# Query and key products in halves with shifted operands, and three reorderings in a two-layer hybrid decoder kernel

## The chip, the cores and the metric

The kernel runs on one core of a Trainium2 chip. The metric is the device time of one execution in microseconds (us), from the first to the last instruction and a little around them. Three executions of the kernel before took 1192.15, 1189.67 and 1191.78 us; their median is 1191.78.

A core has five engines with a queue of instructions each: TensorE (PE in the profile; its loads of the held operand are counted apart as PEld), VectorE (DVE), ScalarE (ACT), GpSimd (POOL) and SyncE (SP), which here only issues DMA transfers. An engine starts its instructions in the order of its queue and waits at each for the results that it needs. TensorE takes both operands from on-chip memory and writes sums into PSUM.

## The reference, cut to what matters

The inputs are one sequence of 512 tokens with 1024 channels and a conditioning vector `c`. There are two layers; each has a token mixer and then a gated feed-forward part with a convolution, and every part is scaled and shifted by three vectors computed from `c`.

```python
def modulate(x, g, shift, scale):
    return rmsnorm(x, g) * (1.0 + scale) + shift

def s5_mixer(h, ...):                      # layer 0
    u = h @ w_in                           # 1024 -> 1024, 64 groups of 16 channels
    ...                                    # complex diagonal state, 64 per group, scanned over the tokens
    y = gelu(y + d_skip * u)
    y = y * sigmoid(y @ w_glu)
    return y @ w_out

def fox_mixer(h, w_in, b_f, w_out):        # layer 1
    proj = h @ w_in                        # queries, keys, values of 16 heads x 64, and 16 gate columns
    ...                                    # F = cumsum(log_sigmoid(gate + b_f))
    s = q @ k.T / 8 + F[t] - F[s]          # causal, softmax over s
    return softmax(s) @ v @ w_out

def conv_ffn(h, w_up, conv_w, conv_b, w_down):
    a, b = split(h @ w_up)                 # 1024 -> 2 x 2816
    return (silu(causal_conv3(a)) * b) @ w_down

for i in range(2):
    h = h + gate * mixer_i(modulate(h, ...))
    h = h + gate * conv_ffn(modulate(h, ...))
return rmsnorm(h, final_g)
```

All data are float32.

## The kernel before, in words

**Layout.** Activations stand transposed: 1024 channels as 8 tiles (`KT`) of 128 partitions, 512 tokens (`S`) as columns. A large product is computed as three matmuls a tile pair: each operand is split into a high part and a remainder (`hi` and `lo`, both in the fast float32 form), and `hi*hi + hi*lo + lo*hi` is summed in PSUM (`mms`, lines 303 to 310). `put_parts` makes them: ScalarE copies the high part (line 287), VectorE subtracts for the low one (line 292). The products at the start of the state-space layer (lines 1144, 1155 and 1175) and the small ones inside it stay plain float32, one matmul a pair.

**Places in memory.** The normalized input of a product is a pair of tiles `a_hi`, `a_lo`, and a table says how many elements of 4 bytes each is shifted from the start of its room: `WHOLE = {"a_hi": 0, "a_lo": 16}` or `HALF = {"a_hi": 48, "a_lo": 0}` (lines 41 and 42). `norm_mod(i, start)` makes the pair; the default is `WHOLE`. `self.odd` shifts the weights' low part by 32 elements. The up projections of both feed-forward parts use `HALF` and `odd`; the attention layer's input, made by `norm_mod(2)`, uses `WHOLE`.

**`product`** (line 312) runs over output tiles `m`. For each it loads and splits the weights, and then issues the 3 x 8 matmuls over the 512 columns at once, or, with `apart`, over the first 256 columns and then over the second. After each `k` it may call `step`; in the attention layer `step` is `unit`, which issues a piece of the attention work (line 1500 and others) that has fallen due at that count. So attention's matmuls stand between the eight `k` of the query and key products, which are the product over `fox_qk`: 16 tiles, two (queries and keys) for a pair of heads.

**The start.** Line 1114 sums squares for the norm over 512 tokens. `s5_params` then computes, on VectorE, small tables of the state-space layer; a helper called `Ew` logs its operations, and `in_turn` puts two logged lists into one stream so that they are spread evenly over each other. Lines 861 to 864 do this with the inverse root of the norm (`inv_root`, which starts by reading the statistics from PSUM, line 410) and with `s5_turns` (sines and cosines brought to other powers). Line 1130 scales the input by root and gain. The shift vector of the modulation is a product of `c` with a weight matrix that is read as 512 KB pieces (`ada_pe`, line 221; `ada_w` in the transfers); `next(shift)` moves this generator on by one piece, and its last call turns the rows into columns (lines 164 and 169). The first input product (line 1144) uses the input without the shift; the shift's part of it is a column, eight matmuls of one column (line 1155), that ScalarE adds while copying the product out (line 1161, `uf`). From the second input product on (line 1175) the input with the shift is used (line 1164).

**The state-space layer** runs in eight steps `m`. For each, `s5_inputs(m)` makes a 128 x 128 kernel matrix on TensorE (lines 984 and 989), adds `dd`, turns it (line 995, `ktt`), copies it (`kt`, line 996), writes it to a DRAM buffer (`s_z`, line 998) whose other rows are zero, and reads it back in 128 shifted copies (`tw`, line 1001): a 128 x 1024 table. Eight copies multiply this by a causal mask into `t` (line 1007 on ScalarE, line 1005 on GpSimd), one for each position `i` in a block of eight tokens. For the last two tables GpSimd takes some of them: `i` = 2, 5 for table 6 and 0, 2, 5 for table 7. `t` is the operand of the output matmuls of line 1061; those of line 1069 add the part that comes from the states, with tables `w` that VectorE makes (line 958). The outputs go through gelu and are split for the gate's product (lines 1193 and 1194).

**Order.** A scheduler, not the order of the calls alone, sets each engine's queue, so moved code may move its neighbours too.

Of the kernel before, what the change touches and what calls it, by code (L numbers as in the profile page):

```python
# [8 lines left out]
F32 = mybir.dt.float32  # L9
F32R = mybir.dt.float32r  # L10
I32 = mybir.dt.int32
AF = mybir.ActivationFunctionType
# [5 lines left out]
P = 128  # L18
D = 1024
KT = D // P  # L20
S = 512
# [9 lines left out]
NH = 16  # L31
# [32 lines left out]
class Trunk:  # L64
# [247 lines left out]
    def product(self, w, ms, nk, x, evac, head=0, tail=0, after=None, ticks=0, halves=HALVES, tail_pool=(), first=None, step=None, apart=False, ready=(), spare=False):  # L312
# [17 lines left out]
        for m in ms[head:len(ms) - tail]:  # L330
            wk = ready[m] if m in ready else self.weights(w[m], nk)
            ps = self.aux.tile([P, S], F32, name="aux") if spare else self.mm.tile([P, S], F32, name="mmp")
            for c in HALVES if apart else (full,):
                for k in range(nk):
                    self.mms(ps[:, c], wk, x, k, nk, c)
                    if step:
                        step()
            evac(m, ps, full)
            self.tick(ticks)
# [462 lines left out]
class S5(Trunk):  # L802
# [37 lines left out]
    def s5_params(self, pool, tp, prm, stats):  # L840
# [23 lines left out]
        in_turn(*logs)  # L864
# [100 lines left out]

    def s5_inputs(self, m):
# [21 lines left out]
        nc.vector.tensor_tensor(turned, pk[:, 0], dd, ALU.add)  # L988
        for a in range(0, H4, 2):
# [5 lines left out]
        nc.tensor.transpose(pk[:, 1], turned, self.ident)  # L995
        nc.scalar.activation(kt, pk[:, 1], AF.Copy)
        z = self.z[m]
        nc.sync.dma_start(z[:P], kt)
# [4 lines left out]
        for i in range(L):  # L1003
            if m >= KT - 2 and i % 3 == 2 or m == KT - 1 and i == 0:
# [79 lines left out]
    def s5(self, i, nxt):  # L1084
# [4 lines left out]
        with ExitStack() as stack:  # L1089
# [3 lines left out]
            with ExitStack() as start:  # L1093
# [12 lines left out]
                with tc.manual_schedule(engines={ENG.PE, ENG.Activation, ENG.DVE, ENG.SP}):  # L1106
# [29 lines left out]
                    for k in range(KT):  # L1136
# [4 lines left out]
                        if k == 6:  # L1141
                            self.s5_consts(keep, tp)
                            self.s5_signs_b()
                        nc.tensor.matmul(ps, w[0][:, k, :], x[:, k], start=(k == 0), stop=(k == KT - 1))
                    next(shift)
# [7 lines left out]
                    col = self.aux.tile([P, 1], F32, name="aux")  # L1153
                    for k in range(KT):
                        last_mm = nc.tensor.matmul(
# [13 lines left out]
            def inputs(m):  # L1169
                if m:  # L1170
                    if m > 1:
                        load_w(m)
                    ps = self.mm.tile([P, S], F32, name="mmp")
                    for k in range(KT):
# [111 lines left out]
class Kernel(S5):  # L1286
# [98 lines left out]
    def fox_heads(self, pool, x):  # L1385
# [27 lines left out]
        self.product(self.io["fox_qk"], range(NH), KT, x, project, ticks=1, step=self.unit)  # L1413
# [100 lines left out]
def build(tc, io, out, stop=None):  # L1514
    with ExitStack() as ctx:
# [6 lines left out]
        x = k.ffn(1, 0, x, k.norm_mod(2), WHOLE_TILES[0], SUMS, True)  # L1522
# [90 lines left out]
```

## Time and profile before

| What | us |
|---|---|
| three executions | 1192.15, 1189.67, 1191.78 |
| median | 1191.78 |
| profiled execution, its own time | 1192.04 |
| its span, first to last instruction | 1190.3 |
| mean granted clock of TensorE | 0.995 |

| Stage | window | TensorE busy |
|---|---|---|
| norm, tables, modulation | 0 to 26.2 | 17.96 |
| first input products | 26.2 to 65 | 37.96 |
| state-space steps | 65 to 140 | 74.72 |
| last two tables and outputs | 140 to 170 | 24.92 |
| gate and output products | 170 to 262 | 91.14 |
| first feed-forward part | 262 to 638 | 375.10 |
| attention: end of the down projection, values, queries and keys, output | 638 to 850 | 210.19 |
| second feed-forward part | 850 to 1190 | 331.89 |

"Busy" counts time in which an engine has an instruction under way. Matmuls overlap, so a busy TensorE may still run at different paces: the pace is the distance between the starts of two matmuls that follow each other. A group's line in the profile gives line, engine, operation, output and inputs, shape and count; behind the bar stand its busy time and the mean of one in ns, and in brackets the idle time of the engine ahead of it and whose result ended it. The chain of waits goes back from the last instruction, at each step to what released it.

### The profile page before, as it was taken

To read this page: it belongs to the slowest core of one execution; us is meant where nothing else is said; L and a number is where in the kernel's file an instruction comes from. 1 tells how busy PE (TensorE), PEld (TensorE's weight loads), DVE (VectorE), ACT (ScalarE), POOL (GpSimd) and SP (SyncE) were. 2 spreads that over 40 slices of the span, in tenths; PEclk is the share of its full clock that TensorE was granted. 3 is DMA by queue.
4 is the path that set the end of the run, shared out by engine and by line. 5 is a ranking of instruction groups with operands and counts; after the bars stand their busy time and mean duration, and the time that the engine had idled before them with its cause. 6 is when DMAs were issued, how large, how long until landed. Compare 5 with 4: busy or idle time off the path is not lost.

```text
span 1190.3 us, 21170 instructions
## 1 busy us (share of the span) xinstructions
PE 1163.9 (98%) x8183; PEld 1016.3 (85%) x8183; DVE 971.6 (82%) x1813; ACT 639.1 (54%) x1137; POOL 108.8 (9%) x162
## 2 busy tenths in 40 slices
PE   7999989999999999999999999999999999999997
PEld 2456677899999999999999788878999989999987
DVE  8899976889887889876676788866999878888855
ACT  2554525446666666665442666554556545555543
POOL 1000110000011111111000433330000000000000
PEclk9999999999999999999999999999999999999999
DMA  9677758833699898887613555523123332333331
GB/s 360 227 245 250 232 179 292 286 117 108 161 250 257 230 252 235 228 246 200 193 54 127 204 194 177 183 76 108 37 89 103 120 108 87 112 123 108 93 89 71
DMA packets 79427, 202.70 MB, mean 170 GB/s; under 512 B 23919, under 2 KB 26191, under 8 KB 78303
## 3 DMA queue, kind: packets, MB, share of 16 engines
q1 hardware_dynamic: 72847, 181.96, 45.9%
q0 software_dynamic: 6192, 18.88, 9.1%
q8 instruction: 64, 1.05, 0.4%
q10 hardware_dynamic: 288, 0.52, 0.1%
q14 instruction: 36, 0.29, 0.1%
HBM read 194.41 MB, written 6.92 MB: 169 GB/s over the span
## 4 chain that ended last, share of the span: by engine, by line
PE 72%; DVE 15%; DMA 6%; issue 3%; ACT 3%; POOL 1%; SPq 0%; DVEq 0%; POOLq 0%; ACTq 0%
PE mmp L308 35%; PE mmp L568 12%; PE aux L568 5%; DVE w_lo L292 4%; PE mmp L1354 3%; PE mmp L1175 3%; DMA raw<-in_w_up 3%; DVE sums L539 2%; PE mmp L1205 2%; DVE conv L622 2%; PE aux L1500 2%; PE aux L1483 1%; PE aux L1061 1%; PE aux L1069 1%; DVE nm_t L539 1%
## 5 line engine op out<-in xcount | busy, mean ns | idle before, releaser
L287 ACT ACTIVATE w_hi<-raw 128x1024 fp32r<-128x1024 f32 (+4 forms) x197 | 173.3, 888 | 126.2 <-PE mmp L308 60.9
L292 DVE TENSOR_TENSOR w_lo<-raw,w_hi 128x1024 fp32r<-128x1024 f32 (+4 forms) x154 | 155.7, 1013 | 30.9 <-ACT w_hi L287 27.0
L308 PE MATMUL mmp<-ghi,w_hi 128*128 128x512 f32 (+1 forms) x392 | 144.1, 368 | 0.0
L308 PE MATMUL mmp<-glo,w_hi 128*128 128x512 f32 (+1 forms) x392 | 143.7, 367 | 0.0
L308 PE MATMUL mmp<-ghi,w_lo 128*128 128x512 f32 (+1 forms) x392 | 143.6, 366 | 0.0
L308 PE MATMUL mmp<-a_hi,w_hi 128*128 128x256 f32 (+1 forms) x440 | 141.0, 323 | 0.0
L308 PE MATMUL mmp<-a_hi,w_lo 128*128 128x256 f32 (+1 forms) x440 | 139.0, 317 | 0.0
L308 PE MATMUL mmp<-a_lo,w_hi 128*128 128x256 f32 (+1 forms) x440 | 138.8, 316 | 0.0
L568 PE MATMUL mmp<-w_hi 128*128 128x256 f32 x420 | 116.6, 278 | 1.4 <-ACT nm_h L575 1.3
L568 PE MATMUL mmp<-w_lo,w_hi 128*128 128x256 f32 x420 | 116.0, 276 | 0.0
L568 PE MATMUL mmp<-w_hi,w_lo 128*128 128x256 f32 x420 | 116.0, 276 | 0.0
L287 ACT ACTIVATE w_hi<-sums 128x1024 fp32r<-128x1024 f32 x78 | 81.8, 1058 | 44.4 <-DVE sums L539 27.8
L292 DVE TENSOR_TENSOR w_lo<-sums,w_hi 128x1024 fp32r<-128x1024 f32 x78 | 94.3, 1218 | 4.6 <-ACT w_hi L287 3.4
L308 PEld LDWEIGHTS mmp<-a_hi,w_hi 128*128 128x128 f32 x440 | 82.2, 188 | 7.1 <-issue 2.6
L308 PEld LDWEIGHTS mmp<-a_hi,w_lo 128*128 128x128 f32 x440 | 82.6, 188 | 6.4
L256 DVE CUSTOM_DVE_ANT_0 ada_raw<-ada_raw,ada_c,rest 128x1024 f32<-128x1024 f32 x64 | 83.5, 1320 | 5.4 <-DMA ada_raw<-in_ada_rows 5.4
L308 PEld LDWEIGHTS mmp<-a_lo,w_hi 128*128 128x128 f32 x440 | 82.8, 188 | 4.6
L308 PEld LDWEIGHTS mmp<-ghi,w_lo 128*128 128x128 f32 x392 | 73.6, 188 | 12.3
L308 PEld LDWEIGHTS mmp<-ghi,w_hi 128*128 128x128 f32 x392 | 73.6, 188 | 11.2
L308 PEld LDWEIGHTS mmp<-glo,w_hi 128*128 128x128 f32 x392 | 73.6, 188 | 11.1
L568 PEld LDWEIGHTS mmp<-w_hi 128*128 128x128 f32 x420 | 78.8, 188 | 2.6 <-ACT nm_h L575 2.6
L568 PEld LDWEIGHTS mmp<-w_lo,w_hi 128*128 128x128 f32 x420 | 78.9, 188 | 0.0
(326 smaller groups left out, 3053.6 us busy)
## 6 DMA issues: line engine op xcount, KB each, us to landing
raw<-in_w_up SPq DMA_DIRECT2D x88, 512.0 KB, 3.7
ada_raw<-in_ada_rows SPq DMA_DIRECT2D x64, 512.0 KB, 4.9
raw<-in_ada_w SPq DMA_DIRECT2D x32, 512.0 KB, 5.9
raw<-in_w_down SPq DMA_DIRECT2D x32, 384.0 KB, 3.9
raw<-in_w_down SPq DMA_DIRECT2D x32, 320.0 KB, 3.5
nf<-nfd SPq DMA_DIRECT2D x8, 1152.0 KB, 5.7
w_lo<-in_w_up POOLq DMA_DIRECT2D x17, 512.0 KB, 8.1
raw<-in_fox_qk SPq DMA_DIRECT2D x16, 512.0 KB, 3.3
```

The costliest lines, as they stand in the source:

```text
L256: nc.vector.tensor_tensor_reduce(w, w, self.crow, 1.0, self.ada_b[:, i, m:m + 1], ALU.mult, ALU.add, self.par[i][:, m:m + 1])
L287: nc.scalar.activation(hi, src, AF.Copy)
L292: self.late = (nc.vector.tensor_tensor(lo, src, hi.bitcast(F32), ALU.subtract).ins,)
L308: self.last_mm = self.nc.tensor.matmul(o, wt, xt[:, cols], start=(k == 0 and n == 0), stop=(k == nk - 1 and n == 2),)
L539: sub = lambda o, u, v, op=ALU.subtract: nc.vector.tensor_tensor(o, u, v, op)
L568: self.last_mm = nc.tensor.matmul(o, wt[:, k], xt[:, k], start=(first and k == 0 and n == 0), stop=(k == H - 1 and n == 2), skip_group_che ...
L622: nc.vector.scalar_tensor_tensor(t[:, d:], ps[:, :S - d], cw[:, 2 - d, f:f + 1], t[:, d:], op0=ALU.mult, op1=ALU.add)
L1061: nc.tensor.matmul(yp[g2][:, k, :], t[:, 2 * k + g2], u[:, g, :], start=(k == 0), stop=False, skip_group_check=True,)
L1175: nc.tensor.matmul(ps, w[m][:, k, :], x[:, k], start=(k == 0), stop=(k == KT - 1))
L1205: nc.tensor.matmul(gps[m], wt, xt[:, k], start=(k == 0 and part == 0 and xt is yhi), stop=(k == KT - 1 and part == 1))
L1354: self.last_mm = nc.tensor.matmul(ps[q, b][:, :n], xt[:, k, tb], wt, start=(k == 0 and i == 0), stop=(k == KT - 1 and i == 2),)
L1500: nc.tensor.matmul(pv[:, c * P:], self.v[:, hp, k, r].rearrange("p t d -> p (t d)"), pp[:, r, c + 3 * k:NB + 3 * k, :].rearrange("p b t -> ...
```

## The change

It has four parts.

1. *Start, VectorE.* The first 13 operations of `s5_turns` are issued ahead of the inverse root; the other ones stay interleaved with it.
2. *Start, TensorE.* The last call of `next(shift)`, which makes the columns, goes ahead of the last of the eight matmuls of the first input product, and the first matmul of the second input product goes into the middle of the eight one-column matmuls (`second` is its PSUM tile, allocated sooner).
3. *Tables.* Turning the kernel matrix, its copy and its write become a helper, `s5_kernel`. For the last table it is called ahead of the transposes of `w1`. Of the copies into `t`, GpSimd keeps `i` = 2, 5 for table 6 and only `i` = 5 for table 7.
4. *Attention.* `fox_qk` is computed in halves (`apart`) with `odd`; `every=2` calls `step` at every second of the sixteen half steps, so that there are still eight calls a tile. The layer's input is made with `HALF`, which shifts the operands of the values' product (line 1354) too.

```diff
@@ product
-    ..., apart=False, ready=(), spare=False):
+    ..., apart=False, ready=(), spare=False, every=1):
...
             for c in HALVES if apart else (full,):
                 for k in range(nk):
                     self.mms(ps[:, c], wk, x, k, nk, c)
-                    if step:
+                    if step and k % every == every - 1:
                         step()
@@ s5_params
         self.s5_turns(pool, tp, co, si, logs[1])
-        in_turn(*logs)
+        in_turn(logs[1][:13])
+        in_turn(logs[0], logs[1][13:])
@@
+    def s5_kernel(self, ps, turned, kt, m):
+        nc = self.nc
+        nc.tensor.transpose(ps, turned, self.ident)
+        nc.scalar.activation(kt, ps, AF.Copy)
+        nc.sync.dma_start(self.z[m][:P], kt)
@@ s5_inputs
         nc.vector.tensor_tensor(turned, pk[:, 0], dd, ALU.add)
+        if m == KT - 1:
+            self.s5_kernel(pk[:, 1], turned, kt, m)
         for a in range(0, H4, 2):
...
-        nc.tensor.transpose(pk[:, 1], turned, self.ident)
-        nc.scalar.activation(kt, pk[:, 1], AF.Copy)
+        if m < KT - 1:
+            self.s5_kernel(pk[:, 1], turned, kt, m)
         z = self.z[m]
-        nc.sync.dma_start(z[:P], kt)
...
-            if m >= KT - 2 and i % 3 == 2 or m == KT - 1 and i == 0:
+            if m == KT - 2 and i % 3 == 2 or m == KT - 1 and i == 5:
@@ s5, first input product
+                        if k == KT - 1:
+                            next(shift)
                         nc.tensor.matmul(ps, w[0][:, k, :], x[:, k], ...)
-                    next(shift)
...
+                    second = self.mm.tile([P, S], F32, name="mmp")
                     for k in range(KT):
+                        if k == KT // 2:
+                            nc.tensor.matmul(second, w[1][:, 0, :], x[:, 0], start=True, stop=False)
                         last_mm = nc.tensor.matmul(col, w[0][:, k, :], self.par[i][:, k:k + 1], ...)
@@ s5, inputs(m)
-                    ps = self.mm.tile([P, S], F32, name="mmp")
-                    for k in range(KT):
+                    ps = second if m == 1 else self.mm.tile([P, S], F32, name="mmp")
+                    for k in range(m == 1, KT):
@@ fox_heads
-        self.product(self.io["fox_qk"], range(NH), KT, x, project, ticks=1, step=self.unit)
+        self.odd = True
+        self.product(self.io["fox_qk"], range(NH), KT, x, project, ticks=1, step=self.unit, apart=True, every=2)
+        self.odd = False
@@ build
-        x = k.ffn(1, 0, x, k.norm_mod(2), WHOLE_TILES[0], SUMS, True)
+        x = k.ffn(1, 0, x, k.norm_mod(2, HALF), WHOLE_TILES[0], SUMS, True)
```

What it does to the queues is shown at three places. A row gives the line, the operation, its output and inputs, and the shape and count; `mmp` and `aux` are PSUM tiles. The lines of the changed kernel have other numbers: 1144 is 1155 there, 1155 is 1168, 1175 is 1188.

TensorE, from the last of the shift's weight pieces (line 221) to the first kernel matrix (line 984), before:

```order
L1144 MATMUL mmp<-a_x,raw 128x512 x2
L221 MATMUL mmp<-raw,sc_85 32x512 x4
L1144 MATMUL mmp<-a_x,raw 128x512 x2
L164 MATMUL aux<-rest 128x8
L169 MATMUL aux<-sel,ada_rows 128x2 x4
L1155 MATMUL aux<-par_96,raw 128x1 x8
L239 MATMUL aux<-rest,sc 8x128
L1175 MATMUL mmp<-a_x,raw 128x512 x10
L984 MATMUL aux<-x,s_cd_133 32x128 x8
```

The same place now:

```order
L1155 MATMUL mmp<-a_x,raw 128x512 x2
L221 MATMUL mmp<-raw,sc_85 32x512 x4
L1155 MATMUL mmp<-a_x,raw 128x512
L164 MATMUL aux<-rest 128x8
L169 MATMUL aux<-sel,ada_rows 128x2 x4
L1155 MATMUL mmp<-a_x,raw 128x512
L1168 MATMUL aux<-par_96,raw 128x1 x4
L1167 MATMUL mmp<-a_x,raw 128x512
L1168 MATMUL aux<-par_96,raw 128x1 x4
L239 MATMUL aux<-rest,sc 8x128
L1188 MATMUL mmp<-a_x,raw 128x512 x9
L992 MATMUL aux<-x,s_cd_133 32x128 x8
```

One matmul of 512 columns now stands between the turned columns (line 169) and the one-column products, and one in the middle of these; the ten that followed are nine.

SP's queue of transfers around the first table (the first `s_z` and the first `tw` are table 0; `u` and `s_ud` belong to the second input product; `ada_w` are weights of the next modulation), before:

```order
L1180 DMA s_ud<-uf 128x512
L978 DMA dd<-in_s_dd 128x128
L998 DMA s_z<-kt 128x128
L192 DMA raw<-in_ada_w 128x1024
L1182 DMA u<-s_ud 128x8x64
L1001 DMA tw<-s_z 128x1024
L998 DMA s_z<-kt 128x128
L978 DMA dd<-in_s_dd 128x128
L192 DMA raw<-in_ada_w 128x1024
```

Now:

```order
L1193 DMA s_ud<-uf 128x512
L986 DMA dd<-in_s_dd 128x128
L192 DMA raw<-in_ada_w 128x1024
L1195 DMA u<-s_ud 128x8x64
L972 DMA s_z<-kt 128x128
L986 DMA dd<-in_s_dd 128x128
L192 DMA raw<-in_ada_w 128x1024
L1010 DMA tw<-s_z 128x1024
L972 DMA s_z<-kt 128x128
```

The first table is now written behind the weights and the second `u` rather than ahead of them, and between its write and its read stand a load of `dd` and a piece of weights.

ScalarE around the last two tables (the first row of `t` is table 6, the second table 7; `w_hi` are weights of the gate), before:

```order
L1007 ACTIVATE t<-tw,rest 128x128 x6
L994 ACTIVATE w_1474<-aux 128x512 x2
L996 ACTIVATE kt<-mmp 128x128
L1036 ACTIVATE cf<-s_mask,s_mag_171 128x2x64 x4
L1228 ACTIVATE w_hi<-raw 128x1024 x3
L1075 ACTIVATE yg<-aux 128x256 x2
L1007 ACTIVATE t<-tw,rest 128x128 x5
L1036 ACTIVATE cf<-s_mask,s_mag_171 128x2x64 x4
L1193 ACTIVATE a_hi<-yt 128x512 x2
```

Now:

```order
L1016 ACTIVATE t<-tw,rest 128x128 x6
L1004 ACTIVATE w_1474<-aux 128x512 x2
L971 ACTIVATE kt<-mmp 128x128
L1045 ACTIVATE cf<-s_mask,s_mag_171 128x2x64 x4
L1241 ACTIVATE w_hi<-raw 128x1024 x3
L1084 ACTIVATE yg<-aux 128x256 x2
L1016 ACTIVATE t<-tw,rest 128x128 x7
L1045 ACTIVATE cf<-s_mask,s_mag_171 128x2x64 x4
L1206 ACTIVATE a_hi<-yt 128x512 x2
```

Two of GpSimd's three copies for table 7 are now ScalarE's, so that it has seven where it had five; the copy of `kt` for the last table stands where it stood, behind the copies of table 6 and of `w`.

More of the change, by code (lines that the diff above doesn't have):

```diff
@@ L310, in mms, with product @@
             )
-    def product(self, w, ms, nk, x, evac, head=0, tail=0, after=None, ticks=0, halves=HALVES, tail_pool=(), first=None, step=None, apart=False, ready=(), spare=False):
+    def product(self, w, ms, nk, x, evac, head=0, tail=0, after=None, ticks=0, halves=HALVES, tail_pool=(), first=None, step=None, apart=False, ready=(), spare=False, every=1):
         ms = list(ms)
```

## The prediction

> **What bounds the kernel now.** I read the page's busy shares and its chain of waits first, to see which engine sets the end.
>
> ```profile
> PE 1163.9 (98%) x8183; PEld 1016.3 (85%) x8183; DVE 971.6 (82%) x1813; ACT 639.1 (54%) x1137; POOL 108.8 (9%) x162
> PE 72%; DVE 15%; DMA 6%; issue 3%; ACT 3%; POOL 1%; SPq 0%; DVEq 0%; POOLq 0%; ACTq 0%
> ```
>
> TensorE is busy 98% of the span and is 72% of the chain, so the change can pay in two ways only: TensorE waits less, or its matmuls follow each other faster. The second needs the pace, which busy time doesn't give (matmuls overlap). I took it from the chain, where a stretch of one kind of matmul has a start, a length and a count, and from the first and last start of an unbroken run in the timeline.
>
> ```profile
> 262.61 48.08 PE mmp L308 x424
> 343.37 8.17 PE mmp L308 x36
> 251.95 2.88 PE mmp L308 x24
> 593.38 3.42 PE mmp L308 x30
> 639.72 0.28 PE L1354 MATMUL mmp<-w_hi,a_lo 128*128 128x256 f32 x1
> ...
> 644.76 0.28 PE L1354 MATMUL mmp<-w_hi,a_lo 128*128 128x256 f32 x1
> ```
>
> Row one is the first up projection: halves of 256 columns, input by HALF, weights at odd places, 113.4 ns each (48.08/424). Row two is a down projection in whole matmuls of 512 columns, 227 ns. So 2 x 113.4 = 226.8: halves cost nothing there. Rows three and four are two tails in halves, of the state-space output (no offsets, 2.88/24 = 120 ns) and of the down projection (own offsets, 114 ns). The last pair is the value product, 42 matmuls in 5.04 us: 120 ns. The same shape thus runs at 113.4 or at 120 ns, and place in memory is what differs.
>
> Then I asked for the granted clock in windows (columns: window, its length, busy time of TensorE, weight loads, VectorE, ScalarE, GpSimd, clock, DMA share, GB/s).
>
> ```profile
> 37.30:40.70 3.40, 3.13 (x25) 2.81 (x26) 3.23 (x10) 1.97 (x5) 0.00 (x0) 1.00 0.01 5
> 40.70:44.10 3.40, 3.40 (x6) 1.34 (x5) 3.33 (x6) 3.40 (x7) 0.00 (x0) 0.50 0.48 124
> 153.35:156.76 3.41, 0.41 (x4) 0.41 (x4) 3.38 (x6) 1.53 (x3) 3.19 (x7) 1.00 0.18 65
> 156.76:160.17 3.41, 3.41 (x13) 2.93 (x12) 1.54 (x3) 0.00 (x0) 0.00 (x0) 0.50 0.28 97
> 180.65:184.06 3.41, 2.55 (x17) 1.99 (x16) 2.24 (x3) 1.39 (x3) 0.00 (x0) 1.00 0.97 339
> 184.06:187.47 3.41, 3.41 (x10) 2.63 (x9) 0.90 (x3) 0.00 (x0) 0.00 (x0) 0.50 1.02 401
> ```
>
> Three times the clock is halved for 3.4 us, each time after 3.4 us in which TensorE streamed little (one-column matmuls, an idle stretch, two matmuls and a wait). Each costs up to 1.7 us. The change touches the places of the first two.
>
> **The start.** Rows: VectorE's turns and norm root, the scaled input, and what TensorE does with it.
>
> ```profile
> 16.78 0.16 DVE L410 TENSOR_SCALAR rs_v<-aux 128x4 f32<-128x4 f32 x1 [1.52 <-PE aux L1119]
> 25.24 0.16 DVE L174 SCALAR_TENSOR_TENSOR ga<-aux,rest 128x8 f32<-128x8 f32 x1
> 25.43 5.36 DVE L1130 SCALAR_TENSOR_TENSOR a_x<-h,ga,aux 128x512 f32<-128x512 f32 x8
> 24.12 1.06 PE L221 MATMUL mmp<-raw,sc 128*32 128x512 f32 x8
> 26.23 1.98 PE L1144 MATMUL mmp<-a_x,raw 128*128 128x512 f32 x4 [1.05 <-DVE a_x L1130]
> 38.22 1.95 PE L1155 MATMUL aux<-par,raw 128*128 128x1 f32 x16 [0.27 <-ACT par L177]
> 40.41 0.69 ACT L1161 ACTIVATE uf<-mmp,u_shift 128x512 f32<-128x512 f32 x1
> 41.15 3.77 ACT L1164 ACTIVATE a_x<-a_x,par 128x512 f32<-128x512 f32 x6
> 108.50 3.49 PE mmp L1175 x8
> 54.66 6.38 DMA tw<-s_z
> 61.06 2.58 ACT t L1007 x8
> ```
>
> VectorE idles 1.52 us for the statistics while work stands behind the waiting instruction. Thirteen short turn instructions fill that gap, so the root and all behind it come up to 1.5 us sooner. The scaled input is waited for by TensorE, idle 1.05 us: it can gain no more than that, and the weights of the shift land only just ahead of their matmuls, so I take 0.85 (bounds 0.5 and 1.05).
>
> Two 512-column matmuls, 0.87 us each (3.49/4), now stand among the parameter columns and the one-column matmuls. No 3.4 us there is empty any more, and if the half clock at 40.7 stays away that is 1.7 us (bounds 0 and 1.7). The 0.27 us wait at 38.22 goes too. The price: the column ends one matmul later, and ScalarE's `uf` and the third input slice stand behind it (from 40.41 to 41.15 + 3.77/6 = 41.78 in the old trace, with a small copy ahead). Where two matmuls covered these 1.4 to 1.6 us, one is left, and TensorE waits some 0.65. Net 0.85 + 1.7 + 0.27 - 0.65 = 2.2.
>
> SP now writes table 0 after the second `u` and reads it after a 128x128 load, which waits for table 1's sum, and a 512 KB weight. The read issued at 54.66 gains some 0.5 instead of 2.2, and the eight copies behind it (2.58 us) set the first output. What covers the rest is the two input matmuls that the change places ahead of that output (1.74 us). I charge 0.2: the start is worth **2.0** (bounds 0.3 and 2.6). From 65 to 140 TensorE hardly waits, so this carries through.
>
> **The last table.** Copies of table 7, the output that needs them, and VectorE's work for the sixth output.
>
> ```profile
> 150.88 1.72 ACT L1007 ACTIVATE t<-tw,rest 128x128 f32<-128x128 f32 x5 [2.06 <-DMA tw<-s_z]
> 151.03 5.26 POOL L1005 TENSOR_SCALAR t<-tw,rest 128x128 f32<-128x128 f32 x3 [8.12 <-DMA tw<-s_z]
> 156.35 1.63 PE L1061 MATMUL aux<-u,t 128*128 128x64 f32 x8 [3.53 <-POOL z_gap L136]
> 153.63 1.26 ACT L1193 ACTIVATE a_hi<-yt 128x512 fp32r<-128x512 f32 x2
> 154.29 1.35 DVE L1194 TENSOR_TENSOR a_lo<-yt,a_hi 128x512 fp32r<-128x512 f32 x2
> 156.76 1.21 DVE L958 TENSOR_TENSOR w<-w,x 128x1024 f32<-128x1024 f32 x1
> 160.88 2.00 PE L1069 MATMUL aux<-ua,w 64*128 64x63 f32 x32
> ```
>
> GpSimd takes 1.75 us a copy, ScalarE 0.32 (2.58/8). Two of three copies move: GpSimd is done at 152.8, ScalarE at 150.88 + 1.72 + 0.64 = 153.2. The output starts there, 3.1 sooner. What is late next: after eight more matmuls (1.8 us) TensorE is at 156.2 and needs `w` of line 958, ready at 157.97. This gets later, since ScalarE's two `a_hi` stand behind the two added copies and VectorE's `a_lo` behind these: about 0.6. So line 1069 starts near 158.6, not 160.88: **2.3** (bounds 0.6, if VectorE slips more, and 3.1). It holds at either clock, since VectorE sets it. "Last table sooner" I cost at nothing: on ScalarE the `kt` copy of table 7 still stands behind six `t` and two `w` copies, and were it sooner, line 958 would still hold the output back.
>
> **The attention layer.** HALF also moves the input of the value product, where it is the loaded operand. Of 288 matmuls of 256 columns, 192 run alone at 120 and may go to 113.4 (1.27 us); 96 run between others of 272 columns. I take **1.5** for all (bounds 0 and 2.4). The query and key products run at this pace now, a pair's bursts between attention work:
>
> ```profile
> 699.11 3.65 PE mmp L308 x15
> 703.41 1.39 PE mmp L308 x6
> 705.46 2.09 PE mmp L308 x9
> 708.42 2.74 PE mmp L308 x12
> ```
>
> The four make 9.86 us for 42, where 226.8 each in halves would make 9.53: 0.33 a pair at most, 2.3 over seven. Part of it is the entry of a burst (the first row alone stands at 243), and entries don't get fewer; the other three stand at 228 to 232. I take **0.6**. At 120 the 768 halves need 92.2 us against 384 x 230 = 88.3: a loss of 3.8, the lower bound. Steps stay eight a tile (every second of sixteen), so attention stays where it was between matmuls.
>
> **Sum.** 2.0 + 2.3 + 1.5 + 0.6 = 6.4, against the profiled execution's own 1192.04: 1185.6. That execution lies 0.26 over the median 1191.78 of runs between 1189.67 and 1192.15; I forecast **1185.5**. The third half-clock stretch (184.06) I leave as it is.
>
> **Rivals.** *The clock gate falls elsewhere.* The three half-clock stretches lie on one grid of 3.41 us (40.70, 156.76 and 184.06 are 34 and 8 steps apart). [...] If it is halved in spite of the change, or the old median missed it already: 1187.2. [...]
>
> *The start is swallowed.* The first table is read no earlier and the loop waits for it: 2.0 goes to 0.3, and the time is 1187.2 again. For it: the SP order; against: TensorE's two matmuls of cover.
>
> *The value product keeps 120*, since its input is loaded and not streamed: 1.5 goes, 1187.0. Against it stand the rows at 251.95 and 593.38: same roles, two paces, so that roles are not what sets the pace. [...]
>
> *The offsets do nothing in this layer:* values at 120 and the halves at 120 too: 1185.5 + 1.5 + 0.6 + 3.8 = 1191.4, no change. For it: 120 is what two of the five quoted stretches in halves show.
>
> *The halves are slower, and the kernel with them.* In the query and key products a 256-column stream must hide a whole weight load, and attention's reads and writes stand beside it. The other terms give 5.8, and 768 x s - 88.3 passes this at s = 122.5 ns. One more step of the size from 113.4 to 120, at 126.7, costs 9.0: 1195.2. Against it: the up projection holds 113.4 over 424.
>
> **How the numbers follow.** Forecast and its neighbourhood (1183.5 to 1186.9) 0.45; the gate elsewhere 0.20; start swallowed 0.10; values at 120 0.07; more than forecast (the third stretch gone too: 1183.8 and less) 0.06; offsets nothing 0.07; slower halves 0.05. About 0.2%, 2.4 us, is what a measurement of this kernel can tell. Faster: 0.45 + 0.20 + 0.07 + 0.06 and 0.06 of the swallowed start, 0.84; same 0.12, from the rest of that, the offsets and a little of the last; slower 0.04. The range from 1181.8 to 1189.5 takes in the bounds of the terms; of the likeliest case alone 1183.5 to 1186.9.
>
> **What would show it.** Right: VectorE's idle before the root falls under 0.3 us; the clock near 40 stays 1.00; the wait ahead of table 7's output falls from 3.53 us to under 1, with a new wait for `w` of some 2 us ahead of the sixth output's state part; the value product's starts lie 0.113 us apart; the projections' starts too. Wrong: a wait over 1.5 us for table 0; a half-clock stretch between 36 and 45; value starts still 0.120 apart; starts over 0.118 apart in the projections.

## The result, and the profile after

The changed kernel takes 1195.27 us (median), against 1191.78 before. The ratio is 1.0029, with a 95% interval from 1.0017 to 1.0041: slower by about 3.4 us, where 1185.5 us and a gain of 6.3 were forecast. The profiled execution took 1194.82 us. One of the nine executions ran at a granted clock of 0.751 and took 1451.29 us; it is not in the ratio. First the page's busy shares and its chain, by engine:

```profile
PE 1163.8 (98%) x8567; PEld 1033.5 (87%) x8567; DVE 968.5 (81%) x1813; ACT 640.4 (54%) x1139; POOL 113.3 (10%) x160
PE 77%; DVE 9%; DMA 5%; ACT 5%; issue 2%; POOL 1%; SPq 0%; DVEq 0%; POOLq 0%; ACTq 0%
```

These rows show no loss: 384 more matmuls (each of 384 became two), the same busy time, the same 98%. One has to follow the same event through both traces. The times are starts of the same instruction, in us.

| event | before | after | after minus before |
|---|---|---|---|
| eighth input product copied out (`uf`) | 134.12 | 131.79 | -2.33 |
| statistics read for the first feed-forward norm | 249.45 | 246.27 | -3.18 |
| last part of the values copied out | 645.49 | 641.40 | -4.09 |
| last of the query and key tiles copied out | 785.33 | 787.91 | +2.58 |
| end | 1190.21 | 1192.88 | +2.67 |

In these two traces the state-space layer gave 3.2 us of the 4.3 forecast for it (2.0 + 2.3). All of the loss is in the query and key products: 6.7 us between two neighbouring rows of the table. A smaller piece of that stretch is the cleanest measure, the fifth to the fifteenth copy-out, which is five pairs of heads. The timeline of VectorE, before and then after (start, length, instruction):

```profile
686.11 0.69 DVE L1406 SCALAR_TENSOR_TENSOR lo<-mmp,hi 128x512 fp32r<-128x512 f32 x1 [0.32 <-ACT hi L1404]
...
777.14 0.69 DVE L1406 SCALAR_TENSOR_TENSOR lo<-mmp,hi 128x512 fp32r<-128x512 f32 x1 [0.32 <-ACT hi L1404]
```

```profile
683.92 0.68 DVE L1419 SCALAR_TENSOR_TENSOR lo<-mmp,hi 128x512 fp32r<-128x512 f32 x1
...
780.76 0.68 DVE L1419 SCALAR_TENSOR_TENSOR lo<-mmp,hi 128x512 fp32r<-128x512 f32 x1
```

91.03 us became 96.84: 1.16 us a pair. TensorE's waits from 645 us to the last pair's end name the place, before and after (what waits, for what; sum, times, longest):

```profile
PE mmp L308 <- DVE lo L292: 0.6, 1, 0.6
PE aux L1453 <- DVE mn L1465: 0.6, 1, 0.6
PE aux L1483 <- POOL s L1474: 0.4, 1, 0.4
```

```profile
PE aux L1498 <- DVE plo L292: 4.8, 6, 0.8
PE aux L1498 <- POOL s L1489: 0.5, 1, 0.5
```

Six times, once in each of the last six of the eight pairs, the transposes of the probabilities for the last query block (line 1498) wait 0.8 us for room that VectorE frees with `plo`. What made `plo` late is in VectorE's timeline. One pair, before:

```profile
722.04 0.17 DVE L1472 RECIPROCAL sm<-sm 128x2 f32<-128x2 f32 x1 [1.12 <-ACT s L1469]
722.52 0.69 DVE L1406 SCALAR_TENSOR_TENSOR lo<-mmp,hi 128x512 fp32r<-128x512 f32 x1 [0.31 <-ACT hi L1404]
723.13 1.30 DVE L256 CUSTOM_DVE_ANT_0 ada_raw<-ada_raw,ada_c,rest 128x1024 f32<-128x1024 f32 x1
...
724.36 1.01 DVE L292 TENSOR_TENSOR plo<-aux,phi 128x256 fp32r<-128x256 f32 x2
725.30 1.21 DVE L292 TENSOR_TENSOR w_lo<-raw,w_hi 128x1024 fp32r<-128x1024 f32 x1
```

The same pair after:

```profile
720.56 0.17 DVE L1487 RECIPROCAL sm<-sm 128x2 f32<-128x2 f32 x1 [1.14 <-ACT s L1484]
721.52 1.23 DVE L292 TENSOR_TENSOR w_lo<-raw,w_hi 128x1024 fp32r<-128x1024 f32 x1 [0.79 <-ACT w_hi L287]
722.66 0.68 DVE L1419 SCALAR_TENSOR_TENSOR lo<-mmp,hi 128x512 fp32r<-128x512 f32 x1
723.26 1.28 DVE L256 CUSTOM_DVE_ANT_0 ada_raw<-ada_raw,ada_c,rest 128x1024 f32<-128x1024 f32 x1
...
724.46 1.95 DVE L292 TENSOR_TENSOR plo<-aux,phi 128x256 fp32r<-128x256 f32 x4
```

The split of later weights (`w_lo`) has changed places with the copy-out of the query tile (`lo`). Before, `plo` began 2.32 us after the reciprocal (724.36 - 722.04); now it begins 3.90 after it. On ScalarE `w_hi` stands ahead of `hi` in the same way. No line of the diff moves these: the scheduler chose another order once the products were in halves. In the queues of two kernels that were not run, halves without offsets have the order swapped too, and whole products with offsets don't. The chain of waits after the change runs through just these instructions:

```profile
720.53 0.96 ACT w_hi L287
721.52 1.23 DVE w_lo L292
722.74 0.60 DVE lo L1419
723.34 1.19 DVE ada_raw L256
724.54 0.35 DVE plo L292
725.03 1.22 PE aux L1498 x8
726.25 2.76 PE mmp L308 x24
```

The last row answers the question of pace: 2.76/24 is 115 ns, half of the 230 that whole matmuls took in such a burst. The halves themselves are as fast as forecast.

### The profile page after: what moved, and what is told of

Its sections match the earlier page's. It is cut to its first block, busy times and chain, and to the rows that moved or that the text cites. A ratio compares the mean times of both kernels' runs of the same rounds, so it can differ in the third digit from the quotient of the medians.

```text
span 1192.9 us, 21947 instructions
## 1 busy us (share of the span) xinstructions
PE 1163.8 (98%) x8567; PEld 1033.5 (87%) x8567; DVE 968.5 (81%) x1813; ACT 640.4 (54%) x1139; POOL 113.3 (10%) x160
## 4 chain that ended last, share of the span: by engine, by line
PE 77%; DVE 9%; DMA 5%; ACT 5%; issue 2%; POOL 1%; SPq 0%; DVEq 0%; POOLq 0%; ACTq 0%
PE mmp L308 37%; PE mmp L568 16%; PE aux L568 6%; PE mmp L1188 3%; PE mmp L1367 2%; DVE w_lo L292 2%; ACT s L1484 2%; PE mmp L1218 2%; DMA raw<-in_w_up 2%; PE aux L1515 2%; PE aux L1070 1%; ACT w_hi L287 1%; PE aux L1078 1%; DVE ada_raw L256 1%; PE aux L1498 1%
## 5 line engine op out<-in xcount | busy, mean ns | idle before, releaser
L308 PE MATMUL mmp<-a_hi,w_hi 128*128 128x256 f32 (+1 forms) x568 | 161.9, 287 | 0.0
L308 PE MATMUL mmp<-a_hi,w_lo 128*128 128x256 f32 (+1 forms) x568 | 159.9, 282 | 0.0
L308 PE MATMUL mmp<-a_lo,w_hi 128*128 128x256 f32 (+1 forms) x568 | 159.8, 282 | 0.0
L308 PEld LDWEIGHTS mmp<-a_hi,w_hi 128*128 128x128 f32 x568 | 106.2, 188 | 3.6 <-issue 2.6
L308 PEld LDWEIGHTS mmp<-a_lo,w_hi 128*128 128x128 f32 x568 | 106.8, 188 | 0.9
L308 PEld LDWEIGHTS mmp<-a_hi,w_lo 128*128 128x128 f32 x568 | 106.7, 188 | 0.9
L287 ACT ACTIVATE w_hi<-sums 128x1024 fp32r<-128x1024 f32 x78 | 81.8, 1058 | 43.2 <-DVE sums L539 23.9
```

Source lines behind the costliest of these rows:

```text
L287: nc.scalar.activation(hi, src, AF.Copy)
L308: self.last_mm = self.nc.tensor.matmul(o, wt, xt[:, cols], start=(k == 0 and n == 0), stop=(k == nk - 1 and n == 2),)
```

## The experiments

Numbers of lines shift by a few from one kernel to the next; the names tell what is meant. The kernel before was run again beside each group of variants (medians 1192.58, 1191.91 and 1191.97 us), so it is the ratios that compare.

### The order alone, undone

In the changed kernel, the weights that take an even tile's buffers are queued behind that tile's copy-out.

```diff
@@ product
-            wk = ready[m] if m in ready else self.weights(w[m], nk)
+            with self.behind(*self.held.pop(m, ())):
+                wk = ready[m] if m in ready else self.weights(w[m], nk)
@@ project, even m
-                nc.scalar.activation(hi, ps, AF.Copy, scale=sc)
+                high = nc.scalar.activation(hi, ps, AF.Copy, scale=sc).ins
...
+                self.held[m + 5] = high, *self.late
```

> The changed kernel with one ordering added: in the query and key products, the weights' split that takes the buffers of an even tile (w_hi on ScalarE, w_lo on VectorE) is queued behind that tile's own copy-out (hi, lo), as it stood before the change. Halves, offsets and everything else stay. Theory 'order': six times ScalarE and VectorE split weights first and copy the query tile out second, so the probabilities' parts (plo) come 0.8 to 1.0 us late; TensorE waits 5.4 us and its transposes go at 136 instead of 109 ns for another 1.1. Undoing it gives back 6 to 6.5 us: about 1189 us (1188.3 to 1189.8), the wait of the transposes for plo falls from 4.8 us to under 0.5, and the stretch from the first to the last copy-out of a query or key tile goes from 138.8 us back to 132.3. Rival 'halves': the smaller matmuls (or the reads at other offsets beside attention) are what costs; then the time stays at 1195 (1194 to 1196) and the stretch at 138 to 139.

It took 1189.75 us, ratio to the kernel before 0.9976 (0.9955 to 0.9996). The loss is gone, as the order theory had it; against the changed kernel it is 6.3 us less (0.9976/1.0029). The waits show where it is not gone completely:

```profile
PE aux L1501 <- DVE plo L293: 1.6, 2, 0.8
PE aux L1471 <- DVE lo L293: 0.8, 1, 0.8
PE aux L1471 <- DVE mn L1483: 0.6, 1, 0.6
```

Two waits of six are left, so "under 0.5" was missed, and the whole stretch of copy-outs is 135.4 us instead of 132.3. They are in the last pairs: there the weights that take the buffers belong to the output projection, and my edit held only those of the query and key products. From the fifth copy-out to the eleventh, where the order was held, a pair took 0.03 us more than in the kernel before.

### The order alone, applied to the kernel before

Whole products, old offsets; only the weights of tile m+5 are issued ahead of the copy-out of tile m.

```diff
+        sooner = {m: self.weights(self.io["fox_qk"][m], KT) for m in range(WB)}
         def project(m, ps, cols):
...
+            if m + WB < NH:
+                sooner[m + WB] = self.weights(self.io["fox_qk"][m + WB], KT)
...
-        self.product(..., step=self.unit)
+        self.product(..., step=self.unit, ready=sooner)
```

> The kernel before, with whole 512-column products and its old offsets, in which only the order is swapped: the weights of tile m+5 are issued ahead of the copy-out of tile m in the query and key products, so that ScalarE and VectorE split weights first in every pair. Theory 'order': slower by 4.5 to 7 us, 1196.3 to 1198.8, with waits for plo of 0.6 to 1.0 us ahead of the transposes of the last query block in six pairs. Rival 'halves': no change, 1191.8 within 1 us.

1197.86 us, ratio 1.0041 (1.0024 to 1.0057), a loss of 4.9 us, and the wait that the kernel before doesn't have:

```profile
PE aux L1487 <- DVE plo L292: 3.6, 5, 1.0
```

Five waits, from the second pair to the sixth: behind tiles 12 and 14 there are no later query or key weights to split. The stretch of copy-outs is 137.3 us. So the order costs this without any half-sized matmul, and the rival that blames the halves falls.

### The attention part undone

```diff
-        self.odd = True
-        self.product(..., step=self.unit, apart=True, every=2)
-        self.odd = False
+        self.product(..., step=self.unit)
...
-        x = k.ffn(1, 0, x, k.norm_mod(2, HALF), ...)
+        x = k.ffn(1, 0, x, k.norm_mod(2), ...)
```

> The changed kernel with its attention part undone (query and key products whole, old offsets, step at every k), the three reorderings kept. Both theories on the attention layer: the loss goes away and the rest stays, 3.2 to 3.9 us under the kernel before, about 1188.2 (1187 to 1189.5); at the norm behind the state-space layer (VectorE's first read of its statistics, 249.45 before and 246.27 changed) it stands within 1 us of 246.3. If instead the reorderings had also set attention's queues, its time would stay over 1191.

1188.09 us, ratio 0.9959 (0.9943 to 0.9975). The three reorderings are worth some 0.4%, and the fifth to fifteenth copy-out take 91.0 us again. The norm behind the state-space layer was reached at 242.56 in this trace, 3.7 us sooner than forecast, although the code ahead of it is that of the changed kernel. GpSimd's copy took 3.80 us there instead of 5.55, TensorE's wait for it was 1.5 us instead of 2.7, and no window of the layer had half the clock. This led to the last table.

### The last table without GpSimd

```diff
-            if m == KT - 2 and i % 3 == 2 or m == KT - 1 and i == 5:
+            if m == KT - 2 and i % 3 == 2:
```

> The changed kernel, with the last of GpSimd's copies for table 7 on ScalarE too (eight there, none on GpSimd). [...] Rival 'number of copies': GpSimd's time doesn't matter, ScalarE's added copy delays a_hi, a_lo and with them w, and the gain is under 0.7 us: 1194.6 to 1195.3.

1189.99 us, ratio to the kernel before 0.9986 (0.9971 to 1.0001); against the changed kernel that is 0.9986/1.0029, or 5.1 us, more than my estimate of 2 to 3.5 (from the wait of 2.71 us ahead of the output, and from the state part of the sixth output, which began at 158.98 and which I held possible at 155.5). But each ratio is uncertain by 0.0012 to 0.0016, and the same edit without the attention part (0.9940, in the last table of this section, against 0.9959) comes to 2.3 us. So that the copy cost something is shown, and a surplus over the expectation isn't. What the copy had cost stands in the chain of waits, of the kernel before and then of the changed kernel:

```profile
147.34 3.51 DMA tw<-s_z
...
151.03 5.26 POOL t L1005 x3
...
156.35 1.63 PE aux L1061 x8
```

```profile
144.44 3.33 DMA tw<-s_z
...
147.95 5.55 POOL t L1014
...
153.56 1.97 PE aux L1070 x8
```

Three copies took 5.26 us and one took 5.55. From the landing of the table to its output were 5.50 us before (147.34 + 3.51 = 150.85 to 156.35) and 5.79 after. Without the copy, TensorE's timeline has no wait there:

```profile
151.04 0.39 PE L1218 MATMUL mmp<-a_lo,w_hi 128*128 128x512 f32 x1
151.27 1.00 PE L1070 MATMUL aux<-u,t 128*128 128x64 f32 x8
...
153.64 2.00 PE L1078 MATMUL aux<-ua,w 64*128 64x63 f32 x32
```

Here the state part of the sixth output (line 1078) began at 153.64. I had taken it to be held until 155.5 by the `w` that VectorE was then making; that `w` is for the seventh. What else this pair of traces differs in is the clock. Windows of the changed kernel (columns as in the prediction):

```profile
149.44:152.85 3.41, 1.41 (x7) 0.80 (x5) 3.41 (x7) 2.73 (x9) 3.41 (x1) 1.00 0.37 129
152.85:156.26 3.41, 2.70 (x10) 2.54 (x11) 2.96 (x5) 0.00 (x0) 0.90 (x5) 0.50 0.54 159
156.26:159.67 3.41, 3.41 (x13) 2.34 (x13) 0.00 (x0) 0.00 (x0) 0.00 (x0) 0.50 0.00 0
```

In the first, which has most of the wait of 2.71 us in it, TensorE was busy for 1.41 us, and in the next two, 6.82 us, the granted clock was 0.50. Whole matmuls started 0.42 to 0.43 us apart there (155.86, 156.29 and 156.71), and 0.22 to 0.24 at a clock of 1.00 (149.76 to 150.45), so that up to half of the 6.82 us, 3.4, is my estimate of what was lost. Without the wait, with all of table 7 on ScalarE, the trace has no half clock in the layer at all. Of the fourteen traces, seven have this wait: six of them, with waits of 1.9 to 3.9 us, show one or two halved windows around its end or behind it, and the one with 1.5 us shows none. So such a wait can cost its length and, by that estimate, another 1.7 or 3.4; what decides between none, one and two halved windows isn't shown. The half clock came without the wait too: of the seven traces without this wait, two have it in the layer (6.83 us from 146.93 in the one of whole products with no GpSimd at table 7, and 13.65 us from 142.91 with only TensorE's start changed).

### GpSimd with three copies again

```diff
-            if m == KT - 2 and i % 3 == 2 or m == KT - 1 and i == 5:
+            if m >= KT - 2 and i % 3 == 2 or m == KT - 1 and i == 0:
```

> The changed kernel with GpSimd taking three copies of table 7 as before the change (i = 0, 2, 5) instead of one. [...] Rival 'number of copies' at 1.75 us each, as the prediction had it: three take 3.5 us more than one, the end goes to 157 and the wait to 6.2 us.

A single execution took 1197.85 us, and the wait ahead of the output was 3.9 us. The single instructions, by line (shortest, middle and longest in ns, first and last start), of this kernel and then of the kernel with only TensorE's start changed, which follows below:

```profile
L1014 POOL TENSOR_SCALAR t<-tw,rest x3: 489/489/5946, 147.5 to 153.7; 128x128 f32<-128x128 f32 x3
```

```profile
L1005 POOL TENSOR_SCALAR t<-tw,rest x3: 504/888/1961, 148.2 to 150.5; 128x128 f32<-128x128 f32 x3
```

The first copy took 5.95 us, the other two 0.49 each, and all were done at 154.15, 0.65 later than one alone, where 1.75 us a copy would have put the end at 157. Taking the shortest, 0.49 us, for the work of a copy, the longest had 5.5 us more, which I count as waiting. For what? In the changed kernel VectorE works without a gap beside the copy, as the window of the copy shows (third pair of numbers):

```profile
147.95:153.50 5.55, 2.90 (x38) 2.12 (x32) 5.55 (x9) 4.22 (x13) 5.55 (x2) 0.94 0.49 135
```

The last VectorE instructions of that window, in its timeline:

```profile
151.86 1.28 DVE L1207 TENSOR_TENSOR a_lo<-yt,a_hi 128x512 fp32r<-128x512 f32 x2
153.06 0.68 DVE L1039 TENSOR_TENSOR m<-aux,s_rot 128x512 f32<-128x512 f32 x1
```

All VectorE instructions of the window that start before 153.06 take their inputs from SBUF, the on-chip memory; `m<-aux` is the first with one in PSUM, and GpSimd's copy ended during it, at 153.50. In the second row's run TensorE was at half clock just then (0.50 from 148.24 to 151.34), VectorE had a gap of 0.31 us, and three copies were done in 3.1 us. But only the first of the three fell into that gap; the other two took 1.96 and 0.89 us beside a VectorE without gaps whose inputs were all in SBUF. All three did so in the trace of the order applied to the kernel before, and were done in 4.1 us (the window's columns as above):

```profile
L1005 POOL TENSOR_SCALAR t<-tw,rest x3: 887/1519/1942, 150.2 to 152.4; 128x128 f32<-128x128 f32 x3
150.23:154.33 4.10, 2.20 (x14) 1.44 (x10) 4.10 (x7) 3.82 (x11) 4.10 (x4) 1.00 0.51 152
```

So an input in PSUM or a gap isn't needed for a copy to get on. What lets it in stays open.

What the traces have in common is this: the copies were long beside VectorE instructions with two inputs in SBUF, and in four of them (the changed kernel, the one with three copies again, the turns alone and the order undone) the long copy, of 5.55 us in the first, 5.95 in the second and 5.81 in the last, ended beside the first input in PSUM. In those four the copy lasted through several VectorE instructions (eight in the changed kernel); in the two above, copies of 0.89 to 1.96 us were done beside such instructions. What VectorE's inputs have to do with it is therefore not shown.

### The start, one part at a time

The first 13 turn operations ahead of the root, alone, on the kernel before:

```diff
-        in_turn(*logs)
+        in_turn(logs[1][:13])
+        in_turn(logs[0], logs[1][13:])
```

> The kernel before with the first part of the change alone: 13 turn operations ahead of the norm root. By the prediction's term VectorE's scaled input starts 0.5 to 1.05 us sooner than 25.43, and the copy-out of the eighth input product (uf, 134.12 before) comes 0.4 to 1.0 sooner. If the half-clock stretch near 40 is what the second part removes, it is still there. If the turns alone made the gain of the start, the copy-out stands at 132 and there is no half clock.

TensorE's part alone (the shift's columns ahead of the last matmul, and one matmul of the second product among the one-column products):

```diff
+                        if k == KT - 1:
+                            next(shift)
                         nc.tensor.matmul(ps, w[0][:, k, :], x[:, k], ...)
-                    next(shift)
...
+                        if k == KT // 2:
+                            nc.tensor.matmul(second, w[1][:, 0, :], x[:, 0], start=True, stop=False)
```

> The kernel before with the second part alone: one 512-column matmul behind the shift's columns and one among the one-column products. If it fills the thin window, no half clock is granted between 36 and 45 and the eighth copy-out (134.12 before) comes 1.0 to 1.9 us sooner; if the half clock there hung on where the grid of windows lies, it can show again.

Single executions took 1191.4 and 1189.12 us. The scaled input started at 24.43 with the turns alone (24.07 in the changed kernel, 25.43 before), and the eighth copy-out came 2.86 us sooner than before, more than the 2.33 of both parts together and near the 132 named for the case that the turns make the gain; with TensorE's part alone it came 1.98 sooner. These are small steps for single traces: the ten traces with both parts put this copy-out between 131.61 and 133.08, and the two with neither at 134.12 and 133.71. So both parts together are worth 0.6 to 2.5 us, and which of them made it these single traces can't tell. In neither trace is the clock halved near 40 us (1.00 from 34.06 to 44.29 with the turns alone). It is halved there before (0.50 from 40.70 to 44.10) and with the order applied to the kernel before (39.8 to 43.2), so of three traces without TensorE's part two have it, and of those with it none. But the trace with the turns alone shows that it also stays away without that part, so I can't give the 1.7 us to it. What TensorE's part costs is seen plainly, in the waits up to 65 us of the turns alone and of the changed kernel:

```profile
PE mmp L221 <- DMA raw<-in_ada_w: 0.4, 2, 0.2
PE aux L1156 <- ACT par L177: 0.3, 1, 0.3
```

```profile
PE mmp L1188 <- ACT a_x L1177: 0.7, 1, 0.7
PE aux L1070 <- ACT t L1016: 0.5, 1, 0.5
```

The wait of 0.3 went and one of 0.7 came, for the third slice of the input with the shift. The 0.5 is the wait for the first table, which the turns alone don't have: its read was issued at 52.71 there and at 55.58 in the changed kernel.

### Offsets

Two variants of the best kernel with halves (below), one without the offsets (the input by `WHOLE`, no `odd`),

> best_halves without the offsets (input and weights where they stood before, no odd): 256-column matmuls whose operands all begin at the same place. If the offsets set the pace of halves, the query and key products go at 120 ns instead of 114 and the 768 of them take 4 to 5 us more between the first and the last copy-out (132.3 to 137), the value product 120 instead of 118. If the offsets do nothing there, the stretch stays at 132 to 133.

and one with the input at other offsets.

```diff
-        x = k.ffn(1, 0, x, k.norm_mod(2, HALF), ...)
+        x = k.ffn(1, 0, x, k.norm_mod(2, {"a_hi": 16, "a_lo": 0}), ...)
```

> best_halves with the attention input at other offsets: a_hi shifted by 16 elements and a_lo by 0 (instead of 48 and 0), so that the two loaded operands of the value product begin at two different places, both other than the streamed one's, as in the tail of the down projection that runs at 114. If it takes three different places to reach 113.4, the value matmuls go at 113.5 to 115 ns and the values' stretch is 0.7 us shorter than with 118. If the loaded operand's place counts less than the streamed one's, they stay at 117 to 118.

Single executions took 1188.64 and 1187.07 us. Without offsets the fifth to fifteenth copy-out took 93.00 us against 91.17 with them, and the stretch of all copy-outs 135.8 against 133.8: offsets matter for halves here, at about half of the 4 to 5 us that I had put on them. For the value product, the last starts of the changed kernel and of the one with other offsets, 45 and 48 matmuls apart:

```profile
635.37 0.28 PE L1367 MATMUL mmp<-w_hi,a_lo 128*128 128x256 f32 x1
...
640.67 0.28 PE L1367 MATMUL mmp<-w_hi,a_lo 128*128 128x256 f32 x1
```

```profile
632.82 0.28 PE L1372 MATMUL mmp<-w_hi,a_lo 128*128 128x256 f32 x1
...
638.26 0.28 PE L1372 MATMUL mmp<-w_hi,a_lo 128*128 128x256 f32 x1
```

5.30/45 is 117.8 ns and 5.44/48 is 113.3; before it was 120. So the offset of the loaded operand did move the pace here, and `HALF` wasn't the right one for this product; by what rule, the runs don't show. For the query and key products it was the better one: with the other offsets their halves started 118 ns apart (median) instead of 114, and the fifth to fifteenth copy-out took 92.30 us against 91.17.

The faster value matmuls also met a wait that the kernel before doesn't have, for VectorE's copy-out `v`; in the trace with the other offsets it is

```profile
627.32 0.38 PE L1372 MATMUL mmp<-w_hi,a_hi 128*128 128x256 f32 x1 [0.58 <-DVE v L293]
```

and 0.2 us in the changed kernel.

### Both repairs together

Whole products as before, with all of table 7 on ScalarE:

> The changed kernel without its attention part (whole 512-column query and key products, old offsets) and with all eight copies of table 7 on ScalarE. If the two findings add up (attention's order costs 6.3 us, GpSimd's last copy 4 to 5): the 1195.3 of the changed kernel less 6.3 to 7.2 less 4 to 5.3, about 1184 us (1182.5 to 1185.5), 0.6 to 0.8% under the kernel before. If the gain without GpSimd was only a half-clock stretch that happened to miss, 1187 to 1188.

Halves with offsets, all of table 7 on ScalarE, and the order held for the last pairs too:

> The changed kernel with halves and offsets kept, all eight copies of table 7 on ScalarE, and the weights' split behind the copy-out for every query tile, the last two pairs too (there the output projection's weights take the buffers). Theory 'order': no waits for plo are left in any pair, and since the pairs with the order restored took as long as whole products did, it stands within 1 us of best_whole: about 1184 us, ahead by 0.3 to 0.4 at most for the value product's 118 instead of 120 ns. If halves with offsets were a gain that the order hid: 1182 or less. If they cost: 1186 or more.

The first of them with the other offsets for the value product:

> best_whole (whole query and key products, all eight copies of table 7 on ScalarE) with the attention input's a_hi shifted by 16 elements and a_lo by 0: whole products run at 227 ns at any offset, and the value product's matmuls should go at 113 to 114 ns instead of 120. That is 192 x 6.6 ns, or 1.3 us, up to 1.9 us if those between 272-column ones gain as well: the stretch from the first to the last values' copy-out falls from 36.2 us to 34.5 to 35.2, and the time to about 1183 (1181.5 to 1184.5). If the offsets slow the query and key products, the stretch from their first to last copy-out rises over 133 us.

| kernel | median, us | ratio to the kernel before, 95% interval |
|---|---|---|
| changed | 1195.27 | 1.0029 (1.0017 to 1.0041) |
| whole, no GpSimd at table 7 | 1184.46 | 0.9940 (0.9927 to 0.9952) |
| halves, order held, no GpSimd at table 7 | 1184.30 | 0.9936 (0.9924 to 0.9948) |
| whole, other value offsets, no GpSimd at table 7 | 1185.37 | 0.9948 (0.9931 to 0.9964) |

All three beat both kernels, and can't be told apart. In their traces the fifth to fifteenth copy-out took 90.97, 91.17 and 91.26 us. With the order held, halves are thus worth nothing in the query and key products, at the right offsets. The other value offsets shortened the stretch from the first to the last copy-out of the values from 36.20 to 35.67 us, not by the 1 to 1.7 that I expected; the same wait of 0.6 us for `v` is in that trace. The stretch of the query and key copy-outs grew from 132.16 to 132.63 us, about as much as the values had gained; that whole products keep 227 ns at any offset is not shown by it.

## Why the prediction was wrong

**The attention layer: the step that failed.** It is "Steps stay eight a tile (every second of sixteen), so attention stays where it was between matmuls." That is true of TensorE's queue, and I took it for the whole layer. The queues of ScalarE and VectorE changed, the query tile's copy-out fell behind a weights' split, and 0.6 us of gain became a loss of 6.7. Undoing that order alone gave back 6.3 us, and applying it alone to the kernel before cost 4.9.

**Its pace was right.** Bursts run at 115 ns a half, as the 230 a whole suggested. The rival "the halves are slower, and the kernel with them" gave 1195.2, which is the time measured, but not by its mechanism: it wanted 126.7 ns. A time that agrees is no evidence for the way to it.

**The start was sized right, for reasons only half right.** 2.0 was forecast and 2.33 measured at the eighth copy-out, which is partly luck of the trace: over the ten with the same start the gain is 0.6 to 2.5. The input comes 1.36 us sooner in this trace (0.85 taken for TensorE's share), but at 24.07 to 25.27 in the ten, against 25.01 to 25.43 in the three without the turns. VectorE's idle ahead of the root is gone, as the sign had it, the 0.65 us price of TensorE's part is the 0.7 seen, and the half clock is gone (1.00 from 36.00 to 42.80). But the 1.7 us credited to TensorE's part for that isn't shown to be its own, and it may have been a loss by itself. The "start swallowed" didn't happen: the first table's copies began 0.46 us sooner, near the 0.5 taken, although the read itself was issued 0.92 us later (55.58 against 54.66), not sooner.

**The last table: the second step that failed.** "GpSimd takes 1.75 us a copy" divided a group's busy time by its count. The three were 3.60, 1.41 and 0.49 us long, and with the shortest, 0.49 us, taken for the work, the rest of the length was waiting, beside a VectorE without a gap. Taking two of three away left the long one. Between the table's landing and its output nothing was gained (5.50 to 5.79 us), where 2.3 was forecast. The wait fell from 3.53 only to 2.71, and the sign that I had named, under 1, didn't appear. The "new wait for `w`" didn't either, because that `w` serves a later output. The 0.85 us by which the layer gained beyond the start are little more than the 0.75 by which the table landed sooner than the start explains (150.85 to 147.77, less 2.33); of half-clock windows there is one more here, and one less at 184.

**The value product.** 1.5 was forecast, 0.26 measured in the stretch of its copy-outs (36.19 to 35.93). That the offset moves the pace was right, but the one in use gave 117.8 ns, not 113.4. At an offset that gave 113.3 the stretch gained 0.57 where 1.27 was reckoned for the matmuls that run alone: TensorE then waited 0.58 us for VectorE's copy-out, a wait that the sum left at nothing. The rival by which the product keeps 120 is out, since the places of the loaded operand moved its pace.

**What stays open.** How much of the start's 1.7 us of clock belongs to TensorE's part; what decides whether a half clock follows a stretch with little work for TensorE, and for how long; what lets a GpSimd copy in beside a busy VectorE; which rule of places sets the pace of halves; and why the scheduler's order tips with halves, of which only that it does is shown.

## What to carry to other kernels

Cutting an instruction in two can change the scheduler's order on other engines, so every engine's queue in that loop has to be read again, above all the order of a copy-out and of work for later tiles; an order that matters is better fixed by an explicit edge than left to come out right. A group's mean hides waits inside instructions: look at shortest and longest before taking the mean as a price. Here GpSimd was a poor helper beside a VectorE that was busy from end to end (0.49 to 5.95 us a copy); the copies went to ScalarE at 0.32 us each (2.58/8 in the prediction) and the kernel gained.

## What was not expected of the hardware

One 128x128 copy on GpSimd took from 0.49 to 5.95 us in these traces, the long ones all beside a VectorE that was busy almost without a gap (5.55 of 5.55 us in the changed kernel). A wait of 3.53 us on TensorE went with 3.41 us at a granted clock of 0.50 in the kernel before (156.76 to 160.17), and a shorter one, of 2.71 us, with 6.82 us in the changed one (from 152.85). And the same 256-column matmuls started 120, 117.8 or 113.3 ns apart by the place in memory of the operand that is loaded, not streamed.
